# Offsetting the weights' low part by 64 bytes and doing six of its steps first, in the seven-product half-pairs of two FFN output projections

## The chip, the cores and the metric

The kernel runs on one core of one Trainium2 chip. The metric is the device time of one execution in microseconds; the time before is the median of three runs.

## What is computed

One decoder layer for 512 tokens of width 1024, in float32: a half-step SwiGLU FFN with pre- and post-norm, a token mixer, and a second half-step FFN.

```python
x = x + 0.5 * rms_norm(swiglu_ffn(rms_norm(x, norm_pre[0]), ffn1_w_in, ffn1_w_out), norm_post[0])
x = x +       rms_norm(token_mixer(rms_norm(x, norm_pre[1]), ...), norm_post[1])
x = x + 0.5 * rms_norm(swiglu_ffn(rms_norm(x, norm_pre[2]), ffn2_w_in, ffn2_w_out), norm_post[2])

def swiglu_ffn(x, w_in, w_out):          # w_in 1024 x 5632, w_out 2816 x 1024
    gate, up = jnp.split(x @ w_in, 2, axis=-1)
    return (jax.nn.silu(gate) * up) @ w_out
```

The change touches the product with `w_out`, once in each FFN.

## The kernel before

**Split products.** Every large operand is split into a high part (rounded to the matmul's float32r type) and a low part (what is left over). A product is three matmul steps: high by high, high by low, low by high (`mm3`, L127 to L131; in the loops the pairs `(0, 0), (0, 1), (1, 0)`). ScalarE makes the high part by a copy with a cast (L232), VectorE the low part by a subtraction (L233). Both are queued in an order written out by hand.

**Where weights lie.** All split weights go through one tile `w` of four slots (`split`, L188). A slot is 2·1024+128 float32 elements of each partition, and the weight's high part (1024 elements, read as `k` blocks) is followed at once by its low part. The slot's start is moved by 64-byte units: `o = PAD + (2*D+128)*n - 16*late`, with `late` 1 for a plain weight of `w_out`, and 2 for a pair's weight and for the pair's sums. `drop` gives a slot back, for the next `split`.

**Input projections.** `prod` (L496, matmul at L509) does an FFN's input projection as seven products of half size for each block of columns (`p1` to `p7`), each of 24 steps of 256 columns: eight high by high, eight with the low part of one operand, eight with that of the other. The weights are the stationary operand (loaded into TensorE by a weight load, PEld), the activations the moving one (`xq` and `sq` tiles). In `p7` the activations' two parts lie in swapped order, and start 64 bytes apart by modulo 512 (`open_ffn`, L482 to L487); in all other products of `p1` to `p6` they start alike. The weights of `c1` and `e1` lie in a third layout, `stay[1]`, with the low part 192 bytes further (`NEAR`, 48 elements).

**Output projections.** `ffn_out` (L696) goes through two halves of 512 output columns. A half has eleven entries in the order of `OUT` (L33), each a pair of 128-row blocks of the hidden dimension. A kind `p` or `r` is plain: `out_mm` does 24 steps of 512 columns (L129 to L131). The kinds `k`, `b` and `s` (three in each half, `k3`, `k4` and `b2`, so six in each FFN and twelve in all) are done by `seven` (L723, matmul at L738): Strassen's scheme with seven products of 256 columns. Here the activations `h` and their sums `hs_` are stationary, 128 tokens at a time, and the weights `w` and their sums `wt` are moving. A product has two token blocks `t` and three steps for each: 7 · 2 · 3 = 42 steps. Products 1, 2 and 3 read `w`, the other four read `wt`; 1, 5, 6 and 7 go to four banks `sums`, the others to the accumulators `acc`. A half's last pair is followed by `gather` (L743, VectorE at L755), which combines the four sums. The order of products is 1, 5, 6, 7, 2, 3, 4, and each step pattern is high by high, high by low, low by high, where the second index is that of the weights:

```python
for m, (x, y) in enumerate(((0, 0), (0, 1), (1, 0))):
    self.nc.tensor.matmul(out, a[:, x, ka, tok(qa, t)], b[:, y, kb, col(qb)], ...)
```

**Addresses.** In the built program all starts of stationary and moving operands of these matmuls are multiples of 64 bytes apart. What differs is the distance from the moving operand's start to the stationary one's, here by modulo 256 bytes. It is 64 in all steps of `seven`, and in all steps of `prod` but two sorts: the middle eight of `p7` (the moving part lies 64 bytes further) and the eight steps of `c1` and `e1` with the weights' low part (the stationary part lies 192 bytes further), where it is 0. In the plain steps of 512 columns it is 0.

Of the kernel before, what the change touches and what calls it, by code (L numbers as in the profile page):

```python
# [16 lines left out]
D = 1024  # L17
# [34 lines left out]
class Load:  # L52


    def __init__(self, key, src, a, b, ring="raw", depth=3, ahead=3, group=None):
        self.key, self.src, self.a, self.b, self.ring, self.depth, self.ahead = key, src, a, b, ring, depth, ahead
        self.group = group


class Item:  # L60

    def __init__(self, key, loads, rows=None, adds=(), dst=None, then=None, late=None, defer=False):
        self.key, self.loads, self.rows, self.adds, self.dst, self.then, self.late = key, loads, rows, adds, dst, then, late
        self.defer = defer
        self.reads = {key, *(k for pair in adds for k in pair)}


class Layer:  # L70
# [26 lines left out]
    def col(self, n=1):  # L97
        return self.sp.tile([P, n], F32, tag=f"col{n}", bufs={1: 12}.get(n, 4), name=self.name("col"))
# [89 lines left out]
    def split(self):  # L188

        nc = self.nc  # L190
        it = self.items.popleft()
        raw = self.raw[it.key]
        _, a, b = raw.shape
        if it.dst:
            w = it.dst()
        else:
            if self.wt is None:
                self.wt = self.wp.tile([P, (2 * D + 128) * WBUF], F32R, name="w")

            n = self.free.popleft()  # L200
            o = PAD + (2 * D + 128) * n - 16 * (it.late if it.late is not None else b == 512)
            w = self.wt[:, o : o + 2 * D].rearrange("p (b k t) -> p b k t", b=2, k=a)
            self.slot[id(w)] = n, w
        hi, lo = self.both(w)
        self.ready.append((w, it.dst is not None))
        rows = it.rows
        if rows is None:
            yield from self.cast(hi, lo, raw, it.defer)
        else:
            for j in range(a):  # L210
                nc.scalar.activation(hi[:, j], raw[:, j], AF.Copy, scale=rows[:, j : j + 1])
            yield
            for j in range(a):
                nc.vector.scalar_tensor_tensor(
                    lo[:, j], raw[:, j], rows[:, j : j + 1], hi[:, j].bitcast(F32), op0=ALU.mult, op1=ALU.subtract
                )
        with self.behind(*self.hold):
            for out, other in it.adds:
                o, c = self.raw[out], self.raw[other]
                nc.gpsimd.tensor_tensor(o, o, c, op=ALU.add)  # L220
        if it.then:
            it.then(raw)
        self.load_due(self.done)
        self.done += 1
        yield
# [375 lines left out]
    def start(self, norm, xn):  # L601
# [8 lines left out]
        split = self.split()  # L610
        step(q[1][0], q[1][1])
        next(split)
        step(q[1][0])
        next(split)
        step(q[0][0], q[1][0])
        head = deque(HEADS)
# [79 lines left out]
    def ffn_out(self, gpost_row, scale, after, trans, head):  # L696
# [5 lines left out]
        made = [len(hs)]  # L702
# [20 lines left out]
        def seven(acc, sums, begun, w, wt, h, hs_, stop):  # L723
            tok = lambda q, t: slice(HALF * q + P * t, HALF * q + P * (t + 1))
            col = lambda q: slice(HALF * q, HALF * (q + 1))
            for p, a, ka, qa, b, kb, qb in (
                (1, h, 0, 0, w, 0, 0), (5, hs_, 1, 1, wt, 0, 0), (6, hs_, 0, 0, wt, 1, 1), (7, hs_, 0, 1, wt, 0, 1),
                (2, h, 1, 0, w, 1, 0), (3, hs_, 1, 0, w, 1, 1), (4, h, 1, 1, wt, 1, 0),
            ):
                fresh = p in sums and p not in begun  # L730
                begun.add(p)
                for t in range(2):
                    if p in sums:
                        out = sums[p][:, col(t)]
                    else:
                        out = acc[2 * (p == 4) + t][:, col(p == 3)]
                    for m, (x, y) in enumerate(((0, 0), (0, 1), (1, 0))):
                        self.nc.tensor.matmul(  # L738
                            out, a[:, x, ka, tok(qa, t)], b[:, y, kb, col(qb)],
                            start=fresh and t + m == 0, stop=stop and m == 2, skip_group_check=True,  # L740
                        )

        def gather(sums, pairs):  # L743
            x, y = (self.hf[:, 2 * k : 2 * k + 2, :].rearrange("p t (c v) -> p t c v", c=2) for k in pairs)
# [13 lines left out]
        n = 0  # L758
        with self.tc.manual_schedule():
            for half in range(2):  # L760
                sums = {p: self.ps() for p in (1, 5, 6, 7)} if half else None
                acc = [self.ps() for _ in range(NT)]
                sums = sums or {p: self.ps() for p in (1, 5, 6, 7)}
                todo = self.outs(half)[: -LAST if half else None]
                begun, terms = set(), None
                fast = [k2 for _, k2, kind in todo if kind in "kbs"]
                for m, k2, kind in todo:
                    more(n + 2)
                    w = self.pull()
                    wt = self.pull() if kind in "kbs" else None  # L770
                    more(n + 3)
                    h, hs_ = hs.popleft()
                    if kind in "pr":
                        for i in range(NT):
                            out_mm(acc[i], w, h, i, m == 0, m == PAIRS - 1 or (half == 1 and i == NT - 1 and m == todo[-1][0]))
                    else:
                        seven(acc, sums, begun, w, wt, h, hs_, k2 == fast[-1])
                        self.drop(wt)
                    self.drop(w)
                    if fast and k2 == fast[-1]:  # L780
                        terms = gather(sums, [k for _, k, kind in self.outs(0) if kind == "k"])
                    n += 1
                    if n == 1:
                        self.prod("p4", PAIRS - 1)
                    elif n == 2:
                        self.after("p4", PAIRS - 1)
                    self.lag()
# [102 lines left out]
    def ffn_items(self, name, w_in, w_out):  # L890

        made = []
        place = {"p1": "a", "p2": "c", "p3": "d", "p4": "a", "p5": "a", "p6": "a", "p7": "b"}
        place.update({"c1": "a", "c2": "c", "c3": "b", "c4": "d"})
        adds = {}
        for t in range(1, PAIRS):
            if t >= HEAD:
                v1, v3 = ("p1", t), ("p4", t - 1)
            elif t > 1:
                v1, v3 = ("p3", t - 1), ("p6", t - 1)  # L900
            else:
                v1, v3 = ("p1", 1), ("p1", 2)
            for at, o, i in ((("p5", t), "a", "d"), (("p6", t), "a", "c"), (v1, "a", "b"), (v3, "b", "d")):
                adds.setdefault(at, []).append(((name, t, o), (name, t, i)))

        def load(t, r, group=None):
            ring = ("raw", 3) if t % 2 == 0 and r != "c" else ("raw2", 5)
            k, c = int(r in "cd"), int(r in "bd")
            c0 = c * FF + t * 2 * P
            src = w_in[k * 4 * P : (k + 1) * 4 * P, c0 : c0 + 2 * P].rearrange("(k p) f -> p k f", p=P)  # L910
            return Load((name, t, r), src, KH, 2 * P, *ring, 8, group)

        own = {("p1", t): [load(t, r) for r in "abdc"] for t in range(2, PAIRS)}
        own["c1", 0] = [load(t, r, None if (t, r) == (0, "d") else name) for t in range(2) for r in "acbd"]

        stay = {"c1": 1, "c3": 2, "c4": 0}
        for p, t in ORDER:
            if p[0] == "e":
                continue
            dst = (lambda n=stay[p]: self.stay[n]) if p in stay else None  # L920
            made.append(Item((name, t, place[p]), own.get((p, t), ()), None, adds.get((p, t), ()), dst))
        for h in range(2):
            for n, k2, kind in self.outs(h):
                src = w_out[k2 * 2 * P : (k2 + 1) * 2 * P, h * 512 : (h + 1) * 512].rearrange("(k p) d -> p k d", p=P)
                key = (name, "out", h, k2)
                made.append(Item(key, [Load(key, src, 2, 512, "raw2", 5, 8)], then=self.w_sums if kind in "kbs" else None, late=1 + (kind in "kbs")))
                if kind in "kbs":
                    made.append(Item(key, (), late=2, defer=True))
                if h == n == 0:
                    made.append(Item((name, PAIRS - 1, "a"), ()))  # L930
        return made
# [736 lines left out]
```

## Time and profile before

| what | value |
|---|---|
| median of 3 runs | 935.06 us (934.9 to 936.83) |
| the profiled execution's own time | 934.93 us |
| its span, first to last instruction | 932.9 us |
| granted TensorE clock over the span | 0.998 |
| matmul steps in `seven` (L738) | 504, of 7239 in all |

A row of the profile's timeline has the start, the time to the end of the last instruction merged into it, the engine, the line, and a count; the time from one row's start to the next row's start, over the count, is the pace of a step. A row for a line's instructions has the shortest, median and longest duration of one. A matmul's duration (some 280 ns for 256 columns) is longer than the pace (under 120 ns), because several are under way at once.

### The profile page before, as it was taken

Reading aid. Unit: us, or ns where it says so; the run is one execution under the profiler, and the core shown is the slowest. Engines: PE = TensorE matmul, PEld = TensorE weight load, DVE = VectorE, ACT = ScalarE, POOL = GpSimd, SP = SyncE. Lnnn points to the kernel's source line nnn. Section 1 sums busy time; section 2 is a strip of 40 time slices with the busy share of each in tenths; the row PEclk is TensorE's granted clock in tenths of the full one; section 3 lists DMA queues with packets and bytes.
Section 4 is the critical chain, followed back from the end, with each engine's and each line's share of the span. In section 5 each row is a group of like instructions: output and inputs, shape, how many; then the busy total and the mean of one; then the engine's idle time right before and its main releaser. Section 6 shows DMA issues by size and latency. Waiting matters only on the chain.

```text
span 932.9 us, 17378 instructions
## 1 busy us (share of the span) xinstructions
PE 921.9 (99%) x7239; PEld 856.8 (92%) x7239; DVE 759.9 (81%) x899; ACT 480.8 (52%) x653; POOL 289.4 (31%) x225
## 2 busy tenths in 40 slices
PE   9999999999999999999999999999999999999997
PEld 7999999999888879998888888999999999988885
DVE  6798999999768766788766665887999999976874
ACT  7644445444544544987753254853545445544441
POOL 3535555662000028000021301354555565100001
PEclk9999999999999999999999999999999999999999
DMA  9243334332323304432423126214324332233302
GB/s 315 92 136 114 113 92 136 118 110 68 109 95 98 106 1 116 113 91 70 137 69 114 46 90 204 90 27 133 114 91 136 114 113 92 68 115 99 104 23 91
DMA packets 81994, 97.14 MB, mean 104 GB/s; under 512 B 4178, under 2 KB 61558, under 8 KB 81915
## 3 DMA queue, kind: packets, MB, share of 16 engines
q1 hardware_dynamic: 81306, 94.44, 33.3%
q8 instruction: 57, 0.93, 0.4%
q0 software_dynamic: 320, 1.06, 0.3%
q10 hardware_dynamic: 288, 0.52, 0.2%
q14 instruction: 23, 0.18, 0.1%
HBM read 93.90 MB, written 2.11 MB: 103 GB/s over the span
## 4 chain that ended last, share of the span: by engine, by line
PE 61%; DVE 1%; POOL 0%; ACT 0%; issue 0%; DVEq 0%; POOLq 0%; ACTq 0%
PE ps L509 23%; PE ps L129 8%; PE ps L131 8%; PE ps L130 8%; PE ps L454 6%; PE ps L738 3%; PE ps L1167 1%; PE ps L464 1%; PE ps L288 1%; PE ps L1437 0%; PE ps L1405 0%; PE ps L1240 0%; PE ps L1206 0%; PE ps L1407 0%; PE ps L1361 0%; PE ps L1430 0%
## 5 line engine op out<-in xcount | busy, mean ns | idle before, releaser
L233 DVE TENSOR_TENSOR w<-raw,w 128x1024 fp32r<-128x1024 f32 x226 | 374.2, 1666 | 60.8 <-ACT w L232 60.4
L232 ACT CAST w<-raw 128x1024 fp32r<-128x1024 f32 x226 | 235.6, 1051 | 269.8 <-POOL raw L220 92.7
L220 POOL TENSOR_TENSOR raw<-raw,raw 128x1024 f32<-128x1024 f32 x80 | 221.1, 2764 | 175.0 <-DVE w L233 164.5
L509 PE MATMUL ps<-xq,w 128*128 128x256 f32 x2016 | 238.0, 277 | 0.0
L509 PEld LDWEIGHTS ps<-xq,w 128*128 128x128 f32 x2016 | 233.6, 188 | 0.2
L509 PE MATMUL ps<-sq,w 128*128 128x256 f32 x1440 | 171.0, 277 | 0.0
L509 PEld LDWEIGHTS ps<-sq,w 128*128 128x128 f32 x1440 | 167.4, 188 | 0.0
L129 PE MATMUL ps<-w,hs 128*128 128x512 f32 x240 | 93.5, 390 | 0.0
L130 PE MATMUL ps<-w,hs 128*128 128x512 f32 x240 | 93.5, 390 | 0.0
L131 PE MATMUL ps<-w,hs 128*128 128x512 f32 x240 | 93.5, 389 | 0.0
L129 PE MATMUL ps<-w,xq 128*128 128x512 f32 x208 | 83.1, 400 | 0.1
L130 PE MATMUL ps<-w,xq 128*128 128x512 f32 x208 | 81.0, 390 | 0.0
L131 PE MATMUL ps<-w,xq 128*128 128x512 f32 x208 | 81.0, 391 | 0.0
L375 POOL TENSOR_SCALAR col<-col 128x1 f32<-128x1 f32 x24 | 9.7, 403 | 204.3 <-ACT junk L374 204.3
L454 PE MATMUL ps<-xq,w 128*128 128x256 f32 x480 | 55.8, 278 | 0.0
L454 PEld LDWEIGHTS ps<-xq,w 128*128 128x128 f32 x480 | 55.4, 188 | 0.2 <-issue 0.2
L131 PEld LDWEIGHTS ps<-w,hs 128*128 128x128 f32 x240 | 45.1, 188 | 9.4
L129 PEld LDWEIGHTS ps<-w,hs 128*128 128x128 f32 x240 | 45.1, 188 | 8.7
L130 PEld LDWEIGHTS ps<-w,hs 128*128 128x128 f32 x240 | 45.1, 188 | 8.7
L131 PEld LDWEIGHTS ps<-w,xq 128*128 128x128 f32 x208 | 39.0, 188 | 8.7 <-DVE xq L295 0.3
L129 PEld LDWEIGHTS ps<-w,xq 128*128 128x128 f32 x208 | 39.1, 188 | 8.6 <-ACT xq L294 0.7
L130 PEld LDWEIGHTS ps<-w,xq 128*128 128x128 f32 x208 | 39.1, 188 | 7.5
(246 smaller groups left out, 1100.8 us busy)
## 6 DMA issues: line engine op xcount, KB each, us to landing
raw<-in_ffn_w_in_dram SPq DMA_DIRECT2D x88, 512.0 KB, 4.5
raw<-in_ffn_w_out_dram SPq DMA_DIRECT2D x44, 512.0 KB, 3.9
raw<-in_w_mix_in_dram SPq DMA_DIRECT2D x28, 512.0 KB, 4.0
raw<-in_w_mix_out_dram SPq DMA_DIRECT2D x8, 512.0 KB, 3.9
out_dram<-xs SPq DMA_DIRECT2D x8, 256.0 KB, 2.1
xs<-in_x_dram SPq DMA_DIRECT2D x6, 256.0 KB, 6.7
gpost<-in_norm_post_dram SPq DMA_DIRECT2D x3, 512.0 KB
gpre<-in_norm_pre_dram SPq DMA_DIRECT2D x2, 512.0 KB, 4.1
```

The lines of the kernel that those rows point to most:

```text
L129: mm(ps, sh, mh, start=start, stop=False, **kw)
L130: mm(ps, sh, ml, start=False, stop=False, **kw)
L131: mm(ps, sl, mh, start=False, stop=stop, **kw)
L220: nc.gpsimd.tensor_tensor(o, o, c, op=ALU.add)
L232: lambda: nc.scalar.copy(hi, src),
L233: lambda: nc.vector.tensor_tensor(lo, src, hi.bitcast(F32), op=ALU.subtract),
L288: self.nc.tensor.transpose(pt[:, c * P : (c + 1) * P], src[:, k * P : (k + 1) * P], self.ident)
L375: nc.gpsimd.tensor_scalar(m, ss, s2 / D, b, op0=ALU.mult, op1=ALU.add)
L454: mm(ps[:, u0:u1], w[:, a, k, :], self.xop(k, b, u0, u1), start=k + n + m == 0, stop=k == ND - 1 and n == 2, skip_group_check=True,)
L464: self.nc.tensor.matmul(ps[:, :HALF], w[:, a, k, :], self.xop(k, b, 0, HALF), start=m + k == 0, stop=m == 2 and k == ND - 1)
L509: self.nc.tensor.matmul(ps[:, c], wb[b][:, k, v], left[d][:, k, :], start=first and a + n + k == 0, stop=n == 2 and k == KH - 1, skip_grou ...
L738: self.nc.tensor.matmul(out, a[:, x, ka, tok(qa, t)], b[:, y, kb, col(qb)], start=fresh and t + m == 0, stop=stop and m == 2, skip_group_c ...
```

## The change

A pair's weight `w` is stored in two pieces: the high part where it was, the low part 16 elements (64 bytes) further on. The sums `wt` are stored as before. In `seven`, the order of the 42 steps becomes: first the six steps of products 1, 2 and 3 with the weights' low part; then the other twelve steps of these three products; then products 5, 6, 7 and 4 in full. The number of steps and their sizes stay.

```diff
-    def __init__(self, key, loads, rows=None, adds=(), dst=None, then=None, late=None, defer=False):
+    def __init__(self, key, loads, rows=None, adds=(), dst=None, then=None, late=None, defer=False, apart=False):
+        self.apart = apart
...
             w = self.wt[:, o : o + 2 * D].rearrange("p (b k t) -> p b k t", b=2, k=a)
+            if it.apart:
+                w = tuple(self.wt[:, v : v + D].rearrange("p (k t) -> p k t", k=a) for v in (o, o + D + 16))
             self.slot[id(w)] = n, w
...
-            for p, a, ka, qa, b, kb, qb in (
-                (1, h, 0, 0, w, 0, 0), (5, hs_, 1, 1, wt, 0, 0), (6, hs_, 0, 0, wt, 1, 1), (7, hs_, 0, 1, wt, 0, 1),
-                (2, h, 1, 0, w, 1, 0), (3, hs_, 1, 0, w, 1, 1), (4, h, 1, 1, wt, 1, 0),
-            ):
...
+            w, wt = self.both(w), self.both(wt)
+            first = ((1, h, 0, 0, w, 0, 0), (2, h, 1, 0, w, 1, 0), (3, hs_, 1, 0, w, 1, 1))
+            then = ((5, hs_, 1, 1, wt, 0, 0), (6, hs_, 0, 0, wt, 1, 1), (7, hs_, 0, 1, wt, 0, 1), (4, h, 1, 1, wt, 1, 0))
+            steps = [(f, 0, 1, t) for f in first for t in range(2)]
+            steps += [(f, x, 0, t) for f in first for t in range(2) for x in range(2)]
+            steps += [(f, x, y, t) for f in then for t in range(2) for x, y in ((0, 0), (0, 1), (1, 0))]
+            last = {(f[0], t): n for n, (f, _, _, t) in enumerate(steps)}
+            for n, ((p, a, ka, qa, b, kb, qb), x, y, t) in enumerate(steps):
+                out = sums[p][:, col(t)] if p in sums else acc[2 * (p == 4) + t][:, col(p == 3)]
+                self.nc.tensor.matmul(
+                    out, a[:, x, ka, tok(qa, t)], b[y][:, kb, col(qb)],
+                    start=p in sums and p not in begun, stop=stop and last[p, t] == n, skip_group_check=True,
+                )
                 begun.add(p)
...
-                made.append(Item(key, [Load(key, src, 2, 512, "raw2", 5, 8)], then=self.w_sums if kind in "kbs" else None, late=1 + (kind in "kbs")))
+                made.append(Item(key, [Load(key, src, 2, 512, "raw2", 5, 8)], then=self.w_sums if kind in "kbs" else None, late=1 + (kind in "kbs"), apart=kind in "kbs"))
```

With the low part 64 bytes further, the distance of the moving start to the stationary one becomes 0 in the six steps done first, and stays 64 in the other 36.

More of the change, by code (lines that the diff above doesn't have):

```diff
@@ L725, in seven @@
             col = lambda q: slice(HALF * q, HALF * (q + 1))
-            for p, a, ka, qa, b, kb, qb in (
-                (1, h, 0, 0, w, 0, 0), (5, hs_, 1, 1, wt, 0, 0), (6, hs_, 0, 0, wt, 1, 1), (7, hs_, 0, 1, wt, 0, 1),
-                (2, h, 1, 0, w, 1, 0), (3, hs_, 1, 0, w, 1, 1), (4, h, 1, 1, wt, 1, 0),
-            ):
-                fresh = p in sums and p not in begun
-                begun.add(p)
[L732 to L741, printed above, removed]
+            w, wt = self.both(w), self.both(wt)
[11 more added lines that the diff above has]
+                )
+                begun.add(p)
         def gather(sums, pairs):
```

## The prediction

> **What bounds the kernel now.** I read the page first: the busy shares, then the chain that ended last.
>
> ```profile
> span 932.9 us, 17378 instructions
> PE 921.9 (99%) x7239; PEld 856.8 (92%) x7239; DVE 759.9 (81%) x899; ACT 480.8 (52%) x653; POOL 289.4 (31%) x225
> PE 61%; DVE 1%; POOL 0%; ACT 0%; issue 0%; DVEq 0%; POOLq 0%; ACTq 0%
> ```
>
> TensorE is busy for 99% of the span, and no other engine has more than 1% of the chain. Then the view of waits, for TensorE alone: what does it still wait for?
>
> ```profile
> PE ps L464 <- DVE w L233: 1.7, 2, 1.0
> PE ps L125 <- POOL ident masks.py:199: 1.6, 1, 1.6
> PE ps L288 <- DVE xn L393: 0.5, 1, 0.5
> PE ps L288 <- DVE hf L393: 0.4, 1, 0.4
> ```
>
> That is 4.2 us in all and nothing at L738. So the time is the number of steps times the pace of a step, and a change that keeps the steps can gain by their pace alone, or lose by a new wait. I took the pace of L738 from a table by window, each window one pair from its first step to the next entry's first:
>
> ```profile
> 239.39:244.33 4.95, 4.95 (x42) 1.00 0.41 135
> 255.21:260.16 4.95, 4.95 (x42) 1.00 0.50 162
> 276.48:281.43 4.95, 4.95 (x42) 1.00 0.05 10
> ```
>
> 42 steps in 4.95 us is 117.8 ns for a step, at the full granted clock (1.00), whatever the DMA does beside it (a share of 0.05 to 0.50). Twelve such pairs are 59.4 us. Is that the pace of any 256-column step? The timeline of L509, the same shape, says no:
>
> ```profile
> 28.13 5.76 PE L509 MATMUL ps<-xq,sq 128*128 128x256 f32 x48
> 33.72 8.64 PE L509 MATMUL ps<-xq,w 128*128 128x256 f32 x72
> 42.20 2.99 PE L509 MATMUL ps<-xq,sq 128*128 128x256 f32 x24
> ...
> 51.07 2.88 PE L509 MATMUL ps<-xq,w 128*128 128x256 f32 x24
> 53.79 5.60 PE L509 MATMUL ps<-sq,w 128*128 128x256 f32 x48
> 59.23 2.88 PE L509 MATMUL ps<-xq,w 128*128 128x256 f32 x24
> ```
>
> From 33.72 to 42.20 lie 72 steps: 117.8 ns each. From 51.07 to 53.79 lie 24, from 53.79 to 59.23 lie 48: 113.3 ns each. Nothing waits in either stretch, and the distance of the operands' starts (64 modulo 256) is the same in both. So there are **two paces**, 4.45 ns apart, and a stretch keeps the one that it is in. What changes it? The view of a line's instructions, in short windows, shows the pace by a matmul's duration (276 ns in a fast stretch, 281 in a slow one). First around `e1`, whose weights have their low part 192 bytes further (its steps 17 to 24):
>
> ```profile
> L509 PE MATMUL ps<-xq,sq x12: 276/276/276, 28.2 to 29.5; 128*128 128x256 f32 x12
> L509 PE MATMUL ps<-xq,sq x8: 277/283/283, 29.8 to 30.7; 128*128 128x256 f32 x8
> L509 PE MATMUL ps<-xq,sq x20: 281/281/281, 31.3 to 33.5; 128*128 128x256 f32 x20
> ```
>
> Then around `p7`, whose moving low part lies 64 bytes further (its steps 9 to 16):
>
> ```profile
> L509 PE MATMUL ps<-xq,w x15: 281/281/281, 45.7 to 47.4; 128*128 128x256 f32 x15
> L509 PE MATMUL ps<-sq,w x6: 280/282/287, 49.3 to 49.9; 128*128 128x256 f32 x6
> L509 PE MATMUL ps<-xq,w x21: 276/276/276, 51.1 to 53.3; 128*128 128x256 f32 x21
> ```
>
> The reader is to see two switches. Both make the distance 0 for eight steps, and those steps are slow. Behind the stationary shift of `e1` a fast stretch has become slow; behind the moving shift of `p7` a slow one has become fast. It is so in the second FFN too:
>
> ```profile
> 623.18 2.99 PE L509 MATMUL ps<-xq,sq 128*128 128x256 f32 x24
> 626.01 2.99 PE L509 MATMUL ps<-xq,w 128*128 128x256 f32 x24
> 628.84 3.00 PE L509 MATMUL ps<-sq,w 128*128 128x256 f32 x24
> 631.67 2.88 PE L509 MATMUL ps<-xq,w 128*128 128x256 f32 x24
> 634.39 5.60 PE L509 MATMUL ps<-sq,w 128*128 128x256 f32 x48
> ```
>
> Slow until 628.84 (2.83 us for 24), then `p7`, then fast (2.72 us for 24).
>
> **The change part by part.** *The offset and the order as a switch.* The change gives each pair six steps with the moving part 64 bytes further, at its start, and then goes back: the likeness of `p7`, but with six steps for eight, and coming from 512-column steps. What does a switch cost? `p7` took 2.83 us; fast it would be 24 x 0.1133 = 2.72, so 0.11 are lost; its eight first steps were still slow (8 x 4.45 ns = 0.036), so the switch itself costs 0.075 us, in the eight shifted steps and the few behind them. For a pair: 42 x 0.1133 = 4.76, and 0.075, is 4.835 us, against 4.95: 0.11 gained. Then the way back to 512 columns:
>
> ```profile
> 225.63 0.40 PE L129 MATMUL ps<-w,hs 128*128 128x512 f32 x1
> ...
> 231.09 2.99 PE L509 MATMUL ps<-xq,w 128*128 128x256 f32 x24
> ```
>
> ```profile
> 297.25 0.39 PE L129 MATMUL ps<-w,hs 128*128 128x512 f32 x1
> ...
> 302.69 5.11 PE L738 MATMUL ps<-w,xq 128*128 128x256 f32 x42
> ```
>
> 24 steps of 512 columns took 5.46 us behind a fast stretch, and 5.44 behind a slow pair. The difference is 0.02 to 0.03, and I charge 0.025. Left are 0.085 us for a pair, and 12 x 0.085 = **1.0 us**. Its bounds: below, no switch at all and six shifted steps at the price of the `e1` steps. By the rows, `e1` and `e3` took 33.72 - 28.13 = 5.59 us; 16 fast steps are 1.81, 24 slow ones 2.83, so the eight took 0.95, or 1 ns a step over slow; by the durations (283 for 281) 2 ns. That loses 12 x 6 x 2 ns = 0.14 us. Above, a pair that is fast from its first step and goes back for nothing: 12 x 42 x 4.45 ns = 2.24 us gained. I take the 1.0, since a moving part shifted by 64 bytes and put back is what `p7` does.
>
> *The order as waits.* The low part of `w` is now wanted by step 1 rather than 2, `hs_`'s high part by step 5 rather than 7; all other operands are wanted later (`wt` by step 19 rather than 7, `hs_`'s low part by step 16 rather than 9). The tightest pair is the one at 255.21:
>
> ```profile
> 245.66 1.23 DVE L233 TENSOR_TENSOR w<-raw,w 128x1024 fp32r<-128x1024 f32 x1 [2.59 <-ACT w L232]
> ...
> 253.90 1.23 DVE L233 TENSOR_TENSOR xq<-hf,xq 128x1024 fp32r<-128x1024 f32 x1
> ```
>
> ```profile
> 252.81 1.05 ACT L232 CAST xq<-hf 128x1024 fp32r<-128x1024 f32 x1 [1.79 <-DVE hf L947]
> ```
>
> `w`'s low part is done at 246.89, 8.3 us ahead. `hs_`'s high part is done at 253.86, wanted at 255.21 + 4 x 0.118 = 255.68: 1.8 us to spare for 2.05 before. Its low part is done at 255.13, wanted at 256.98 for 256.15 before: the narrowest margin grows from 1.0 to 1.85 us. No wait comes; the cover is that slack, and without it a late `hs_` would cost its lateness once a pair.
>
> *Buffers.* `w` has its last reader at step 18 rather than 36, but `wt` at 42 as before, and `wt`'s slot is given back first, so the next cast waits as it did. ScalarE and VectorE only would gain, and TensorE does not wait for them there. The sums 5, 6 and 7 close 12 steps (1.4 us) later. VectorE combines them while the pair still runs:
>
> ```profile
> 280.09 0.68 DVE L755 TENSOR_TENSOR u<-ps,hf 128x512 f32<-128x512 f32 x1
> ```
>
> That pair began at 276.48. Product 6, which this row reads, now closes at step 30, 276.48 + 30 x 0.118 = 280.0, just when VectorE comes to it, and 7 at step 36, 280.7, for a later row. A few tenths of a us of lateness may come; queued behind are casts of weights such as the one above with its 8.3 us to spare, and TensorE goes on to plain steps. No DMA is moved: the loads are due by item, as before. I set both at 0.
>
> *Sum.* 934.93 - 1.0 = 933.9 against the profiled execution, which lies 0.13 below the median of 935.06. Put on the median that is **934.0 us**, 0.11% faster.
>
> The Trainium skill, page "SBUF — State Buffer", section "SBUF: two separate sides", says that PE never waits on anyone at its SBUF ports. By that a 64-byte offset moves nothing, and the sum would be 0. The trace does not agree within TensorE itself: the same line and shape has 276, 281 and 283 ns by where its operands start and what ran before. I go by the rows, and keep the rule as a rival.
>
> **The rivals.** (1) *The switch does not take.* For it: six steps are fewer than eight, and the pair comes from 512-column steps whose distance is 0 already, so the six steps may run on in the state that made the pair slow; behind the shift of `e1` the stretch ended slow. Against: `p7` ended fast in both FFNs. Price: the 0.14 us above, 935.2.
>
> (2) *Slower: the shifted steps leave disorder.* If the pair stays at the pace of the switch itself: 0.075 us over some twelve steps is 6.2 ns over fast, 1.8 over slow; 42 steps are 0.076 us, and with 0.025 for the way back, 12 x 0.1 = 1.2 us: 936.3. It decides where the mean step behind the first six is over 117.8 ns. Against it: every stretch at distance 64 that I see settles on one of the two paces.
>
> (3) *Fast from the first step*, no price on either side: 2.24 us, 932.8. For it: the 512-column steps run at distance 0 too, so nothing shifts when the pair begins. Against: no 256-column stretch at distance 0 is fast.
>
> (4) *The change does not do what it says*, the pace does not hang on the offset: 935.1. The two ports' rule above would give this. Against: the rows around `p7`.
>
> (5) Beside each of them: the pace of a stretch behind a stall can fall out otherwise.
>
> ```profile
> 606.21 2.99 PE L509 MATMUL ps<-xq,w 128*128 128x256 f32 x24
> ```
>
> From 606.21 to 628.84 lie 192 steps at 117.9 ns, in a part whose likeness in the first FFN began fast (the 276 ns from 28.2 on). Fast, they would save 192 x 4.45 ns = 0.85 us; other such stretches are as large in the other direction.
>
> **How the numbers follow.** The forecast has 0.55, (1) 0.16, (2) 0.12, (3) 0.12, (4) 0.05. About 0.2% (1.9 us) is what a measurement of this kernel can tell from no change. The forecast alone stays within it, and passes it with the 0.85 of (5), for which I take 0.13 of its 0.55; (3) passes it by itself. Faster: 0.13 + 0.12 = 0.25. Slower is (2) with the 0.85 against it, 0.07 of its 0.12. The same is the rest: 0.42 + 0.16 + 0.05 + 0.05 = 0.68. The range goes from 932.7, under (3), to 935.8, which is (1) or (4) with most of the 0.85; left out are (2), and (3) with the 0.85 to its good, some 0.15 together.
>
> **What would show it.** Right: L738 in four windows at some 4.84 us for 42, durations of 276 from about the tenth step on and 280 to 287 before; 24 steps of 512 columns behind a pair at 5.46; no wait at L738. Wrong: 281 throughout (1, 4), 276 from the first step (3), over 281 to the last (2), or a wait of L738 for L233. A median beyond 935.8 would say that the switch costs more than it gives, one under 932.7 that something besides the pairs became fast.

## The result and the profile after

| | before | changed |
|---|---|---|
| median | 935.07 us (9 runs, 934.9 to 937.26) | 933.4 us (9 runs, 932.9 to 933.64) |
| profiled execution | 934.93 us, span 932.9 | 932.9 us, span 930.8 |

The ratio is 0.9977, with a 95% interval of 0.9968 to 0.9986: 1.7 us less by the medians. A second measurement, below, gave 1.4; its ratio leaves out one slow run of eleven (948.89 us at a granted clock of 0.948).

The views that answer to those of before come in the same order. TensorE's waits, in the changed kernel (its lines up to L738 are numbered up to three higher):

```profile
PE ps L467 <- DVE w L236: 1.7, 2, 1.0
PE ps L126 <- POOL ident masks.py:199: 1.6, 1, 1.6
PE ps L291 <- DVE xn L396: 0.5, 1, 0.5
PE ps L291 <- DVE hf L396: 0.3, 1, 0.3
PE ps L512 <- ACT xq L311: 0.2, 1, 0.2
```

Nothing waits at L738, as before. Then three pairs by window, from a pair's first step to the next entry's first:

```profile
238.73:243.54 4.81, 4.81 (x42) 1.00 0.41 135
254.43:259.25 4.81, 4.81 (x42) 1.00 0.47 167
275.58:280.39 4.81, 4.81 (x42) 1.00 0.02 6
```

4.81 us for 42 steps, against 4.95. Where in a pair the time went shows in the durations of the first pair, in three windows: the six shifted steps, the next few, the rest. A view counts each step that is under way in its window, so the second row has the last two shifted steps once more, and the third begins with the tenth step.

```profile
L738 PE MATMUL ps<-w,xq x6: 278/283/284, 238.7 to 239.3; 128*128 128x256 f32 x6
```

```profile
L738 PE MATMUL ps<-w,xq x6: 277/283/287, 239.2 to 239.8; 128*128 128x256 f32 x6
```

```profile
L738 PE MATMUL ps<-w,xq x32: 276/277/277, 239.8 to 243.3; 128*128 128x256 f32 x32
```

All were 281. Now most of the shifted steps and of the few behind them take 283 and more, and from 239.8 on the steps have the 276 to 277 ns of the fast stretches. From one step's start to the next, the first ten of this pair took 114, 118, 120, 120, 120, 120, 121, 122, 116 and 114 ns, and the other 32 had the pace of 113.3. The way back to 512 columns, 24 steps between two pairs:

```profile
296.10 0.39 PE L130 MATMUL ps<-w,hs 128*128 128x512 f32 x1
```

```profile
301.55 0.88 PE L738 MATMUL ps<-w,xq 128*128 128x256 f32 x6
```

5.455 us, for 5.440 before, and so behind each of the twelve pairs. The stretch from the first pair's first step to the last matmul of the program, taken from the two traces, went from 686.446 to 685.005 us: **1.44 us less**. Another 0.66 of the 2.1 between the profiled spans lies ahead of any pair: the first pair began at 238.73 rather than 239.39. It was there by the 200th matmul, which started at 30.83 us rather than 31.49, and comes from the loads, norms and first products at the start. In the other kernels below with the same steps up to there, that moment lay anywhere from 30.95 (the changed kernel again) to 32.1, so the 0.66 is not the change's.

### The profile page after: what moved, and what is told of

Its sections match the earlier page's. It is cut to its first block, busy times and chain, and to the rows that moved or that the text cites. A ratio compares the mean times of both kernels' runs of the same rounds, so it can differ in the third digit from the quotient of the medians.

```text
span 930.8 us, 17376 instructions
## 1 busy us (share of the span) xinstructions
PE 919.6 (99%) x7239; PEld 854.7 (92%) x7239; DVE 761.0 (82%) x899; ACT 480.5 (52%) x653; POOL 290.1 (31%) x225
## 4 chain that ended last, share of the span: by engine, by line
PE 61%; DVE 1%; POOL 0%; ACT 0%; issue 0%; DVEq 0%; POOLq 0%; ACTq 0%
PE ps L512 23%; PE ps L130 8%; PE ps L132 8%; PE ps L131 8%; PE ps L457 6%; PE ps L738 3%; PE ps L1168 1%; PE ps L467 1%; PE ps L291 1%; PE ps L1438 0%; PE ps L1406 0%; PE ps L1241 0%; PE ps L1207 0%; PE ps L1408 0%; PE ps L1362 0%; PE ps L1431 0%
```

## The experiments

**The theory**: a run of steps whose moving operand is 64 bytes off, and the return from it, put TensorE into the faster of two paces, which it then keeps to the end of the pair. **Rivals**: the order alone does it; the place of the low part alone does it; it takes all six steps, or their place straight behind the 512-column steps. The kernel before, run beside them, had a median of 934.91 us in experiments 1 to 4 and of 935.02 in 5 to 7. Where a kernel ran once, the verdict rests on the pairs of its trace: in each trace all twelve agree within 0.002 us.

**1. The order without the offset** (`order_only`).

```diff
-                w = tuple(... for v in (o, o + D + 16))
+                w = tuple(... for v in (o, o + D))
```

> The changed order, but the weights' low part lies right behind the high part, as before. Theory (switch: six steps at distance 0, then back to 64, put the pair into the fast pace): no shifted step, so no switch; all 42 steps at 117.8 ns, 281 ns each, 4.95 us a pair, about 935.0 us. Rival (the order alone does it, by grouping steps that read the same part): 4.81 us a pair as in the changed kernel, about 933.5.

The first pair by window, and the durations of all steps:

```profile
239.59:244.54 4.95, 4.95 (x42) 1.00 0.42 137
```

```profile
L738 PE MATMUL ps<-w,xq x336: 280/281/282, 239.6 to 898.7; 128*128 128x256 f32 x168
```

934.84 us (ratio to before 0.9998, 0.9988 to 1.0007). From the first pair's first step to the last matmul it took 686.47 us, for 686.45 before. The order alone is worth nothing, and costs no wait.

**2. The offset without the order** (`offset_only`): the products 1, 5, 6, 7, 2, 3, 4, with the steps of each as before.

```diff
-            steps = [(f, 0, 1, t) for f in first for t in range(2)]
-            steps += ...
+            p1, p2, p3, p5, p6, p7, p4 = *first, *then
+            steps = [(f, x, y, t) for f in (p1, p5, p6, p7, p2, p3, p4) for t in range(2) for x, y in ((0, 0), (0, 1), (1, 0))]
```

> The 64-byte offset, but the steps in the order of before, so that a shifted step stands alone between two unshifted ones (steps 2 and 5 of products 1, 2 and 3). Theory (switch): one shifted step may be enough, then the pair is fast behind it and the later shifted steps cost some ns each, 4.82 to 4.88 us a pair and 933.5 to 934.3; or it takes several in a row, then the pair stays slow, 4.95 to 4.98 us and 935.0 to 935.4. Rival (the place of the low part by itself sets the pace, in any order): 4.81 us, 933.4.

```profile
240.01:244.95 4.95, 4.95 (x42) 1.00 0.41 127
```

```profile
L737 PE MATMUL ps<-w,xq x336: 277/281/285, 240.0 to 899.1; 128*128 128x256 f32 x168
```

934.86 us (0.9998, 0.9989 to 1.0008). A shifted step that stands alone disturbs its neighbours (277 to 285) and leaves the median at 281. So neither half of the change does anything by itself, and the place of the low part as such sets no pace.

**3. 128 bytes** (`off128`): `o + D + 32`.

> The changed order with the low part 128 bytes further instead of 64 (distance 192 by modulo 256 in the six steps). Theory (switch, and what counts is the distance by modulo 128): the six steps are no different from the others, no switch, 281 ns throughout, 4.95 us a pair, about 935.0. If the distance counts by modulo 256, the six steps are something new, and may be slower or faster than 117.8. Rival (the place of the low part by itself, anything but adjoining): 4.81 us a pair, 933.4.

```profile
239.61:244.56 4.95, 4.95 (x42) 1.00 0.39 136
```

4.95 us, and 935.09 us in one run. The six steps took 119, 118, 120, 118, 118 and 117 ns, and the one behind them 115; no switch. A low part that is merely not adjoining does nothing. A distance of 192 behaves here nearly like one of 64, which would fit a count by modulo 128; experiment 7 does not bear that count out.

**4. Four shifted steps** (`four_steps`): only the low part of the second block row is moved.

```diff
+                lo = self.wt[:, o + D : o + 2 * D + 32].rearrange("p (k t) -> p k t", k=a)[:, :, : D // 2]
+                w = self.wt[:, o : o + D].rearrange("p (k t) -> p k t", k=a), lo
```

> The changed kernel, but the low part of a weight's first block row stays adjoining and only that of the second is 64 bytes further: of the six steps done first, two are unshifted and the next four shifted. Theory (switch): two steps at 117.8, four shifted ones near 120, then fast: 4.81 to 4.83 us a pair, 933.4 to 933.7. Rival (it takes all six, or it must start with the first step behind the 512-column steps): stays slow, 4.95 to 4.97 us, 935.0 to 935.3.

```profile
239.21:244.02 4.81, 4.81 (x42) 1.00 0.40 132
```

933.26 us in one run. Two unshifted steps, four shifted, and it switches for the same price. The six are not needed, and nor is the place behind the 512-column steps. Two or three shifted steps were not tried.

**5. The six behind the twelve others** (`six_later`).

```diff
+            steps = [(f, x, 0, t) for f in first for t in range(2) for x in range(2)]
+            steps += [(f, 0, 1, t) for f in first for t in range(2)]
```

> The changed kernel, but the six shifted steps come behind the twelve other steps of products 1, 2 and 3 and not ahead of them. Theory (switch: shifted steps, then back): twelve steps at 117.8 ns, the six near 120, a few for settling, then fast: 42 steps in 4.87 us a pair, 0.05 more than the changed kernel's 4.81, some 934.0 us. Rival (it works only ahead, straight behind the 512-column steps, whose distance is 0 too): slow throughout, 4.95 to 4.97 us, 935.0 to 935.2.

The first pair, and its durations in a window ahead of the six and in one behind them:

```profile
239.68:244.55 4.87, 4.87 (x42) 1.00 0.41 134
```

```profile
L738 PE MATMUL ps<-w,xq x10: 281/281/281, 239.7 to 240.7; 128*128 128x256 f32 x10
```

```profile
L738 PE MATMUL ps<-w,xq x27: 276/276/286, 241.1 to 244.1; 128*128 128x256 f32 x27
```

Slow ahead of the shifted steps, fast behind them, in one pair: 4.87 us, and 934.37 us in one run. The switch is where the shifted steps are.

**6. No return** (`all_zero`): `late` 1 for a pair's weight and its sums, nothing apart, so all 42 steps have distance 0.

> The order of the changed kernel, with the pair's weights and sums all moved by 64 bytes and the low part adjoining: distance 0 in all 42 steps, so nothing is put back. Theory (the return makes the pair fast, distance 0 by itself is slow): first step near 114, the rest at 120 ns: 5.03 us a pair, 12 x 0.08 = 1.0 us over the kernel before, about 936. Rival (the pair is fast because its moving operand starts like that of the 512-column steps): 4.76 us a pair, 932.8.

```profile
239.74:244.77 5.03, 5.03 (x42) 1.00 0.42 139
```

```profile
L738 PE MATMUL ps<-w,xq x39: 277/283/283, 239.7 to 244.3; 128*128 128x256 f32 x39
```

936.65 us in one run. Behind a first step of 114 ns all are at 120. Starting like the 512-column steps makes a pair slower than before; apart from that first step, the fast pace is seen only in steps at distance 64.

**7. The heads** (`near0`, `near16`). The rows of before had shown the opposite switch behind `e1`, in the head: the first products of an input projection, up to the first `p7`. In it runs of eight transposes (L291) lie between some products; they are the stalls that the expectations speak of. Like `e1`, `c1` has eight steps with the weights' low part 192 bytes further. Two kernels on top of the changed one alter `NEAR` alone, to 0 and to 16 elements:

```diff
-RAW, WBUF, PAD, LATE, NEAR = 3, 4, 128, 112, 48
+RAW, WBUF, PAD, LATE, NEAR = 3, 4, 128, 112, 16
```

> The changed kernel, and in both FFN heads the low part of c1's and e1's weights adjoins (NEAR 0 for 48), so that their eight steps keep distance 64. Theory (a stationary shift leaves a slow stretch, without a shift a stretch keeps its pace): no steps of 283 ns in the heads, and the stretches behind c1 and e1 keep the pace that the last stall left: between nothing and 1.1 us less in each FFN, 931.5 to 933.4. Rival (the heads are slow for another reason, such as the transposes between): 933.4 as the changed kernel.

> The changed kernel, and in both FFN heads the low part of c1's and e1's weights lies 64 bytes further instead of 192 (distance 128 by modulo 256, 0 by modulo 128). Theory (the distance counts by modulo 128, and a stationary shift leaves a slow stretch whatever its sign): eight steps near 120, then slow as now: 933.4. Rival (the sign of the shift decides, and plus 64 leaves a fast stretch as the moving shift does): durations of 276 from e1 on up to p7, 0.6 us less in each FFN, about 932.2.

The first gave 932.3 us (0.9975, 0.9964 to 0.9985), the second 931.88 (0.9967, 0.9954 to 0.9979). In the first head, first the changed kernel, then `near0`, then `near16`:

```profile
27.39 5.83 PE L512 MATMUL ps<-xq,sq 128*128 128x256 f32 x48
33.06 8.64 PE L512 MATMUL ps<-xq,w 128*128 128x256 f32 x72
41.54 2.99 PE L512 MATMUL ps<-xq,sq 128*128 128x256 f32 x24
```

```profile
27.26 5.60 PE L512 MATMUL ps<-xq,sq 128*128 128x256 f32 x48
32.70 8.32 PE L512 MATMUL ps<-xq,w 128*128 128x256 f32 x72
40.86 2.88 PE L512 MATMUL ps<-xq,sq 128*128 128x256 f32 x24
```

```profile
28.03 5.66 PE L512 MATMUL ps<-xq,sq 128*128 128x256 f32 x48
33.52 8.32 PE L512 MATMUL ps<-xq,w 128*128 128x256 f32 x72
41.68 2.88 PE L512 MATMUL ps<-xq,sq 128*128 128x256 f32 x24
```

The 72 steps between the second row and the third took 8.48, 8.16 and 8.16 us: 117.8, 113.3 and 113.3 ns each. Without a shift of 192 bytes the stretch keeps the fast pace it had, as the theory of `near0` said. `near16` came out as its rival said, and not as its theory: by modulo 128 its shifted steps are at distance 0, like those of the changed kernel (by modulo 256 they are at 128), and yet they left a fast stretch fast. So the distance by modulo 128 is not what decides; whether it is the sign of the shift or its size (64 bytes for 192), no run tells apart. In the second FFN `near0` stayed slow and `near16` was fast: from the start of the row at 604.83 (604.03, 604.75) to that of `p7`'s row at 627.46 (626.64, 626.56), the changed kernel took 22.63, `near0` 22.61 and `near16` 21.81 us.

```profile
604.83 2.99 PE L512 MATMUL ps<-xq,w 128*128 128x256 f32 x24
...
627.46 3.00 PE L512 MATMUL ps<-sq,w 128*128 128x256 f32 x24
```

```profile
604.03 2.99 PE L512 MATMUL ps<-xq,w 128*128 128x256 f32 x24
...
626.64 3.00 PE L512 MATMUL ps<-sq,w 128*128 128x256 f32 x24
```

```profile
604.75 2.88 PE L512 MATMUL ps<-xq,w 128*128 128x256 f32 x24
...
626.56 2.94 PE L512 MATMUL ps<-sq,w 128*128 128x256 f32 x24
```

**8. All three side by side** (`after_again`, `near16_again`, `near0_again`).

> The changed kernel once more, beside the next two. Theory (twelve pairs give 1.45 us): 1.3 to 1.6 us under the kernel before by medians; the time to the 200th matmul, which lies ahead of any pair, may differ by some tenths. Rival (part of the 1.67 us between the first medians was the start of the execution falling out better, by itself): near 1.0.

> The changed kernel with the low part of c1's and e1's weights 64 bytes further instead of 192. Theory (this shift keeps a fast stretch fast, the one of 192 bytes made it slow): 0.5 to 2.0 us under the changed kernel beside it, by how many of the stalls in the two heads are followed by a fast stretch. Rival (the first three rounds were luck): within 0.3 us of it.

> The changed kernel with the low part of c1's and e1's weights adjoining. Theory (no shift, no switch, a stretch keeps the pace of the last stall): 0.5 to 2.0 us under the changed kernel, and within 0.5 of the one with 64 bytes. Rival (the offset of 64 bytes itself speeds the heads up): the latter is faster by 0.5 us and more.

| kernel | median, us | against before at 935.1 | ratio, 95% interval |
|---|---|---|---|
| changed | 933.71 | 1.4 less | 0.9986 (0.9977 to 0.9995) |
| `near0` | 932.93 | 2.2 less | 0.9976 (0.9967 to 0.9985) |
| `near16` | 932.4 | 2.7 less | 0.9967 (0.9954 to 0.9979) |

The changed kernel's gain stands, at the size that its pairs explain. `near16` is the fastest measured, 1.3 us under the changed kernel by medians; their intervals overlap by 0.02%. Between `near0` and `near16` the intervals overlap by half, and the 0.53 us between their medians lies at the border of 0.5 that the expectation drew. But the second head was fast in both profiles of `near16` and slow in all eleven profiles of the other kernels, `near0`'s two among them, so it goes with the offset of 64 bytes. How is open: in `near16` the pace turned fast at a run of transposes (601.14 to 601.93), not at shifted steps, and at the run before it the others turned fast and `near16` did not.

## Why the prediction was right

**The bound.** TensorE's pace was the bound, and nothing else moved: no wait at the matmul of `seven` in any of these traces, and `order_only` at 0.9998 confirms the 0 for waits, buffers and sums together. (The narrowest margin, by the prediction's own figures, grew to 1.82 us, that of `hs_`'s high part, and not to 1.85; nothing hung on it.)

**The switch.** The likeness to `p7` held in all twelve pairs; experiments 1 to 6 show that it needs the offset of 64 bytes and more than one shifted step together (four are enough), and that the steps become fast once they are back at distance 64. In these experiments only the pairs' moving operand was moved, so they do not tell the distance to the stationary one from the place of the moving one alone. The Trainium skill, page "SBUF — State Buffer", section "SBUF: two separate sides", says that PE never waits on anyone at its SBUF ports. What the prediction drew from that rule, that a 64-byte offset moves nothing, did not come true: the same 42 steps take 4.81, 4.95 or 5.03 us by the placing and order of their operands. Whether anything waits at a port in them, no view shows.

**The sum: the size was off.** The term "0.075 us for the switch itself" measured 4.812 - 4.760 = 0.052. It was taken from `p7` with its eight shifted steps and charged to six: in the second FFN of the kernel before, those eight ran at 120.0 ns and the eight behind them at 116.7, together 0.08 us over the fast pace. In a pair the first shifted step ran at 113 to 114 ns, and the price ended with the tenth step. The term of 0.025 for the way back measured 0.015, the 5.455 against 5.440 above. A pair itself went from 4.947 to 4.812 us, and 12 x (0.135 - 0.015) = 1.44 is what the traces show. So a pair gained 0.12 rather than 0.085, and twelve gained 1.44 rather than 1.0. The measured 933.4 lies 0.6 under the forecast of 934.0, in the range; 0.44 of this is the mis-sized prices, and the rest is luck of the size by which a start differs.

**The rivals.** (1), no switch, fell with the twelve pairs at 4.81 us, and (4), no effect of the offset, with `order_only`, which is the changed kernel without it. (2), disorder, did not come; `all_zero` shows what stays at distance 0: 1.6 us over before in its one run, and 1.28 from the first pair's first step on, near the 1.2 that (2) had, by another way. (3), fast from the first step, was seen for one step, and not more. (5) did not decide: the second head of the changed kernel was as slow as before (22.63 us for the same 192 steps). In `near16` that stretch is fast, and shorter by 0.82 us, where (5) had put 0.85.

**The chances.** The two ratios, 0.9977 and 0.9986, lie on either side of the 0.2% that the text called the limit, and the interval of each holds 0.998. "Within 0.2%" was the likeliest, and the 1.44 us that the pairs explain, 0.15%, lie within.

## What to carry to other kernels

When one engine is busy for 99% of the span, it is worth looking for two paces of the same instruction: the time from one row's start to the next, over the count, in several stretches. Here the pace is a state that a stretch keeps, set by what ran just before, so a few steps with another alignment ahead of the rest were worth more than one alignment throughout: either of the two, kept throughout, was slower (4.95 and 5.03 us for 4.81). And undo each half of such a change alone: here neither half did anything.

## What the hardware showed that was not expected

- A state with memory: with the same distance (64 by modulo 256) the same steps run at 113.3 or 117.8 ns, and a stretch keeps its pace over more than a hundred steps. At distance 0 throughout they run at 120 (experiment 6). The distance is not the whole rule: the eight shifted steps of `p7`, at distance 0 as well, took 120.0 ns behind a slow stretch and 117.6 behind a fast one (the second FFN of the kernel before and of `near16`).
- What a shift leaves behind depends on the operand that moved and on how far: four shifted steps or more of the moving operand by 64 bytes left a fast stretch (`p7`, and all pairs of the changed kernel), eight of the stationary one by 192 bytes left a slow one behind a fast one (`c1` and `e1` in the first FFN), and eight of the stationary one by 64 bytes left a fast stretch fast and a slow one slow (`near16`: the first product of the second FFN had 118 ns on both sides of them).
- What makes the two paces is open. That two streams of reads inside TensorE, the weight load and the moving operand, hit each other was only argued: no view shows a port or a bank. A moving offset of 192 bytes was not tried, as the last of the four slots has no room for it.
